# Splitting banded attention probabilities before the turn, and turning them by DMA

## The chip, the cores and the metric

The kernel runs on one core of a Trainium2 chip. A core has five engines with a queue of instructions each: TensorE (PE; its weight loads are shown apart as PEld), VectorE (DVE), ScalarE (ACT), GpSimd (POOL) and SyncE (SP), which here only issues DMAs. An engine works through its queue in order and waits on semaphores for others. The metric is the device time of one launch in microseconds (us), as the median of several runs; lower is better.

## What is computed

One decoder layer on x of 2048 x 1024 floats, with two attention branches side by side. Cut to what matters here:

```python
h = rms_norm(x, g_pre) * (1 + scale) + shift          # scale, shift, gate from silu(c) @ w_ada
qa, ka, va, fa, za, qb, kb, vb, zb = split(h @ w_in)
oa = forgetting_attention(qa, ka, va, fa + b_fgate) * silu(za)      # 8 heads, causal, full length
ob = sliding_window_sink_attention(rope(qb), rope(kb), vb, sinks) * silu(zb)
y  = concat([oa, ob]) @ w_out
out = x + gate * rms_norm(y, g_post)
```

The change is in the second branch, the banded one: 8 query heads, 2 key heads, head size 64. A query of block n (128 queries) sees the 128 keys that end with its own, so keys of blocks n-1 and n, and a learned sink takes part in the softmax but adds no value:

```python
s = q @ k.T / 8                       # 128 queries x 256 keys, per block and head
s = where(band, s, -inf)              # 0 <= i + 128 - j < 128
p = softmax(concat([s, sink]))[:-1]
out = p @ v
```

## The kernel before, in words

Products of floats are made on TensorE from fp16 halves: a number is split into a high half (rounded to fp16) and a low half (the remainder in fp16), and three products (high-high, high-low, low-high) are summed in PSUM.

The work runs in stages. First come the modulation, the normalised input and its first projections. Then comes the stage of the change: from about 139 to 400 us TensorE works off projection units (`punits`, by `fill`, L1185), and between them the banded attention of 32 windows (`Pair`, L932; `windows`, L1182). A window is one pair of query heads and two query blocks, so four blocks of 128 x 128 probabilities. The long causal branch and the output projection follow after the stage.

The order of instructions is written out by hand under a manual schedule. `fill(n)` emits n projection units and what is due at their numbers. `after(n, f)` puts off f by n ticks, and `tick()` (L205) emits what has come due; thus an evacuation by ACT or DVE is put into its queue some units after the matmuls that it waits for. The loop over windows is at L1220. Each turn of it has four parts of projection units (`part`, L1223) and four ticks:

- first tick, then for this window `maxima` (L951): DVE folds the banded scores of 2 blocks x 2 heads, which lie in PSUM, into 128 columns, because each query uses only 128 of its 256 keys (L956), puts in the sink (L958), and takes the row maxima (L961, L963).
- part 0 of the units, then `turn` (L973) for the window before; second tick.
- `exps` (L965): ACT makes four blocks of 128 x 129 exponentials in SBUF in `sm_`, queries on the partitions, with their sums (L970). Part 1, third tick.
- `pv` (L998) two windows back: 24 matmuls (L1005) with the probabilities, keys on the partitions, as stationary operand; later `out_` (L1009) scales by the reciprocal of the sums and stores through `o_store` (L295; ACT high half L307, DVE low half L303, GpSimd issues the store L304 or L297).
- part 2, fourth tick, part 3, then `scores` (L940) of the next window: 12 matmuls (L948) into the single buffer `pss`.
- ACT squares a piece of w_out (L1244) and SP loads the next piece (L1248).

`turn` brings the probabilities to keys on the partitions: TensorE turns the four float32 blocks into the PSUM tile `px` (L977). One tick later (`split`, L985) ACT copies `px` to fp16 as the high half of `fold` (L986), DVE makes the low half as the difference (L987) and the reciprocal of the sums (L989), and GpSimd makes from `fold` the tiles of the two key blocks: four selects (L991, L993) that keep one triangle each and set the other to zero, as the folded columns belong to the previous block above the diagonal and to the own block below it. `fold` and the even windows' result tiles are in the pool `ptp` with one buffer each; odd windows use the pool `stp`. `sm_` is in the pool `sws` with two buffers, `px` in the PSUM pool `ps_t`.

Beside this run in the same stage: the rope of the banded queries (L801 to L829: ACT copy L807, four DMAs on SP that exchange halves L809, DVE products L812, L822, L823, split L826 and L816), the gates (L397: ACT L406, DVE L402, GpSimd store L404), values (L385, L389) and the weight loads and splits (L216 to L293), whose DMAs GpSimd issues.

Much later, at the end of the kernel, the output projection loads stored halves of the attention output with a transposing DMA on SP, 128 x 1024 fp16 each, from DRAM to SBUF (L1555).

Of the kernel before, what the change touches and what calls it, by code (L numbers as in the profile page):

```python
# [10 lines left out]
F32 = mybir.dt.float32  # L11
F16 = mybir.dt.float16
# [3 lines left out]
AF = mybir.ActivationFunctionType  # L16
ALU = mybir.AluOpType
AX = mybir.AxisListType

P = 128  # L20
# [4 lines left out]
CH = 512  # L25
# [18 lines left out]
def hybrid_layer(  # L44
# [17 lines left out]
    V, A, G, PE, SP = nc.vector, nc.scalar, nc.gpsimd, nc.tensor, nc.sync  # L62
# [5 lines left out]
    PSUM = bass.MemoryType.PSUM  # L68
# [14 lines left out]
    def sm(n, tag):  # L83
        return small.tile([P, n], F32, tag=tag, name=tag)
# [70 lines left out]
    ident = const.tile([P, P], F32, name="ident")  # L155
# [46 lines left out]
    def after(n, f):  # L202
        late.append([n, f])

    def tick():  # L205
        now = [f for n, f in late if n <= 1]
        late[:] = [[n - 1, f] for n, f in late if n > 1]
        for f in now:
            f()
# [237 lines left out]
    def turn(ci, k, px=None, us=range(4), hi_a=False):  # L447

        px = px or ps_x.tile([P, CH], F32, tag="x", name="px")

        def turned_(us):
            for u in us:
                PE.transpose(px[:, u * P:(u + 1) * P], xt[ci * 4 + u][:, k * P:(k + 1) * P], ident[:])  # L453

        turned_(us)
        hf = hst.tile([P, CH], F32, tag="hf", name="hf")
        hi, lo = hT[ci][:, 0, k, :], hT[ci][:, 1, k, :]

        def scaled():
            for dst in ([hi] if k % 2 == 0 or hi_a else []) + [hf[:]]:  # L460
                A.activation(dst, px[:], AF.Identity, scale=Gp[:, k:k + 1], bias=Shp[:, k:k + 1])

        def split():
            if k % 2 and not hi_a:
                V.tensor_copy(hi, hf[:])
            V.tensor_tensor(lo, hf[:], hi, op=ALU.subtract)

        return scaled, split, turned_

    def turn_x(ci, k):  # L470
        scaled, split, _ = turn(ci, k)
        after(1, scaled)
        after(2, split)
# [10 lines left out]
    st = start.enter_context(tc.tile_pool(name="start", bufs=1, reuse_waits="tile"))  # L484
# [3 lines left out]
    with ExitStack():  # L488
        rows = st.tile([32, P], F32, name="rows")
# [190 lines left out]
        ada_dve(0, KT - 1, False, 2)  # L680
        ada_sum(0, True)
        turned = [turn(0, k, None, (0, 1)) for k in range(5)]
        squares(0, (2,))
        root(0, slice(2, 3))
# [16 lines left out]
        for u in (2, 3):  # L701
            for k in range(5):
                turned[k][2]((u,))
        turned += [turn(0, k, bk[k - 4]) for k in (5, 6)]
        ku = proj_units("kb", 0, lambda ps, free: kb_units(0, ps, free))
        for k in range(KT):
# [75 lines left out]
    def swa_pool(name, bufs, **kw):  # L782
        return swa.enter_context(tc.tile_pool(name=name, bufs=bufs, reuse_waits="tile", **kw))
# [3 lines left out]
    stp = swa_pool("stp", 2)  # L787
# [144 lines left out]
    class Pair:  # L932
# [39 lines left out]

        def turn(self):  # L973

            px = ps_t.tile([P, 4, P], F32, tag="t", name="pxb")
            for n in range(4):
                PE.transpose(px[:, n, :], self.sm_[:, n, 1:P + 1], ident[:])  # L977
            even = (8 * self.j + self.i // 2) % 2 == 0
            self.ptt = [ptp.tile([P, 2, 4, P], F16, tag=f"pt{b}", name="ptb") if even else
                        stp.tile([P, 2, CH], F16, tag="st", name="ptb") for b in range(2)]  # L980
            ptt = [t[:].rearrange("p a (n c) -> p a n c", n=4) if not even else t[:] for t in self.ptt]
            self.ptt = ptt
            fold = ptp.tile([P, 2, 4, P], F16, tag="fo", name="fold")

            def split():  # L985
                A.activation(fold[:, 0], px[:], AF.Copy)  # L986
                V.tensor_tensor(fold[:, 1], px[:], fold[:, 0], op=ALU.subtract)  # L987
                self.rinv = sm(4, "b_ri")
                V.reciprocal(self.rinv[:], self.rs[:])  # L989
                for n in range(2):  # L990
                    G.affine_select(ptt[0][:, n], fold[:, n], [[0, 4], [-1, P]], ALU.is_ge, 0.0,  # L991
                                    base=-1, channel_multiplier=1)
                    G.affine_select(ptt[1][:, n], fold[:, n], [[0, 4], [1, P]], ALU.is_ge, 0.0,  # L993
                                    base=0, channel_multiplier=-1)

            after(1, split)

        def pv(self):  # L998
            j, i = self.j, self.i
# [182 lines left out]
    windows = [Pair(j, i) for j in range(4) for i in range(0, NB, 2)]  # L1182
    pos = [0]

    def fill(n, each=None):  # L1185

        for _ in range(n):
            for f in events.pop(pos[0], []):
                f()
            punits[pos[0]]()  # L1190
            pos[0] += 1
            if each:
                each()
# [8 lines left out]
    with swa_order:  # L1202
        fill(N_PRO - 4, tick2)
        psx.close()
        sws = swa_pool("sws", 2)
        ptp = swa_pool("ptp", 1)
        ps_s = swa_pool("ps_s", 1, space=PSUM)
        ps_t = swa_pool("ps_t", 1, space=PSUM)
        ps_pv = swa_pool("ps_pv", 1, space=PSUM)
        wsp = swa_pool("wsp", 2)  # L1210
        wss, wst = sm(16, "a_m"), sm(2, "wst")
        wsq = {}
        base = N_PRO
        NW = len(windows)
        windows[0].scores()
        windows[0].maxima()
        fill(2, tick2)
        windows[0].exps()
        fill(2, tick2)
        for n, wd in enumerate(windows):  # L1220
            goal = base + (N_SWA - base) * (n + 1) // NW
            todo = goal - pos[0]
            part = [todo * (m + 1) // 4 - todo * m // 4 for m in range(4)]  # L1223
            tick()
            if n:
                wd.maxima()
            fill(part[0])
            if n:
                windows[n - 1].turn()
            tick()  # L1230
            if n:
                wd.exps()
            fill(part[1])
            tick()
            if n > 1:
                windows[n - 2].pv()
            fill(part[2])
            tick()
            fill(part[3])
            if n + 1 < NW:  # L1240
                windows[n + 1].scores()

            if n:
                A.activation(wsq[n - 1][:], wsq[n - 1][:], AF.Square, accum_out=wss[:, (n - 1) % 16:(n - 1) % 16 + 1])  # L1244
            if n == 16:
                V.tensor_reduce(wst[:, 0:1], wss[:], axis=AX.X, op=ALU.add)
            wsq[n] = wsp.tile([P, 2 * P], F32, tag="wsq", name="wsq")
            SP.dma_start(wsq[n][:], w_out0[n // 4 * P:(n // 4 + 1) * P, n % 4 * 2 * P:(n % 4 + 1) * 2 * P])  # L1248
        tick()
        fill(5)  # L1250
        windows[NW - 1].turn()
        tick()
        fill(5)
        windows[NW - 2].pv()
        tick()
        fill(6)
        windows[NW - 1].pv()
        tick()
        tick()
        A.activation(wsq[NW - 1][:], wsq[NW - 1][:], AF.Square, accum_out=wss[:, 15:16])  # L1260
        V.tensor_reduce(wst[:, 1:2], wss[:], axis=AX.X, op=ALU.add)
        wsum = sm(1, "w_mx2")
        V.tensor_reduce(wsum[:], wst[:], axis=AX.X, op=ALU.add)
# [16 lines left out]
    stp = foxl.enter_context(tc.tile_pool(name="stpa", bufs=3, reuse_waits="tile"))  # L1280
# [432 lines left out]
    with tc.manual_schedule():  # L1713
# [35 lines left out]
        for s, stp_ in enumerate(steps):  # L1749
# [16 lines left out]
            a = b = 0  # L1766
# [102 lines left out]
```

## Time and profile before

| | us |
|---|---|
| median of 3 runs | 1131.02 (1130.87 to 1131.43) |
| the profiled execution | 1129.92 |
| its span, first to last instruction | 1128.2 |
| PE busy in it | 1110.6 |
| DVE busy | 905.6 |
| ACT busy | 656.8 |
| POOL busy | 224.6 |

A line of the timeline holds start and length in us, then engine, line of the kernel, operation, output <- inputs, shapes and how many; in square brackets is the idle time of the engine before it and who ended it. A line of a group holds busy us and the mean of one in ns, then the idle time before. A line of one source line's or tile's view holds the shortest, median and longest of its instructions in ns. Waits are listed as who waited <- for whom: us in total, times, longest. Queue rows end in q (SPq, POOLq): these are issues. DMA rows hold the number, KB of each, and the median us from issue to landing.

### The profile page before, as it was taken

Reading aid. Unit: us, or ns where it says so; the run is one execution under the profiler, and the core shown is the slowest. Engines: PE = TensorE matmul, PEld = TensorE weight load, DVE = VectorE, ACT = ScalarE, POOL = GpSimd, SP = SyncE. Lnnn points to the kernel's source line nnn. Section 1 sums busy time; section 2 is a strip of 40 time slices with the busy share of each in tenths; the row PEclk is TensorE's granted clock in tenths of the full one; section 3 lists DMA queues with packets and bytes.
Section 4 is the critical chain, followed back from the end, with each engine's and each line's share of the span. In section 5 each row is a group of like instructions: output and inputs, shape, how many; then the busy total and the mean of one; then the engine's idle time right before and its main releaser. Section 6 shows DMA issues by size and latency. Waiting matters only on the chain.

```text
span 1128.2 us, 25138 instructions
## 1 busy us (share of the span) xinstructions
PE 1110.6 (98%) x9854; PEld 652.4 (58%) x9854; DVE 905.6 (80%) x1988; ACT 656.8 (58%) x1145; POOL 224.6 (20%) x343
## 2 busy tenths in 40 slices
PE   7899999999999999999999999999999999999997
PEld 2566555676756856556555555655556565544444
DVE  8897488878887468898998989988897997766663
ACT  3974345555555412666766667676666889543332
POOL 3111145545556420010010111001000000100000
PEclk9999999999999999999999999999999999999999
DMA  9854434413333142244223333224311245797632
GB/s 364 280 154 96 81 103 90 93 53 92 83 80 89 39 93 51 65 103 44 58 72 74 86 57 87 51 52 71 72 39 46 76 142 164 153 258 213 193 127 102
DMA packets 124653, 119.77 MB, mean 106 GB/s; under 512 B 66009, under 2 KB 102274, under 8 KB 124534
## 3 DMA queue, kind: packets, MB, share of 16 engines
q1 hardware_dynamic: 113662, 85.66, 28.4%
q0 software_dynamic: 10720, 32.46, 12.6%
q8 instruction: 77, 1.26, 0.6%
q14 instruction: 42, 0.34, 0.1%
q10 hardware_dynamic: 152, 0.04, 0.0%
HBM read 64.43 MB, written 25.18 MB: 79 GB/s over the span
## 4 chain that ended last, share of the span: by engine, by line
PE 83%; DVE 9%; DMA 3%; ACT 3%; issue 2%; SPq 0%; POOL 0%; DVEq 0%; POOLq 0%; ACTq 0%
PE bk L361 32%; PE bk L1650 14%; PE bk L379 7%; PE sta L1414 5%; PE sta L1415 5%; PE bk L1365 5%; PE poa L1440 3%; PE poa L1441 3%; PE poa L1438 3%; PE bk L854 2%; DMA wa<-in_w_ada_dram 2%; PE pss L948 2%; PE pob L1005 1%; PE px L453 1%; DMA xt<-in_x_dram 1%
## 5 line engine op out<-in xcount | busy, mean ns | idle before, releaser
L1421 ACT ACTIVATE p<-sta,lift,scl_qk 128x1024 f32<-128x1024 f32 (+2 forms) x160 | 171.8, 1074 | 128.1 <-PE sta L1415 78.9
L361 PE MATMUL bk<-hT,wh_qk 128*128 128x512 f16 x768 | 196.4, 378 | 0.0
L1428 DVE TENSOR_TENSOR pha<-p,pha 128x1024 f16<-128x1024 f32 (+2 forms) x160 | 168.9, 1056 | 0.2 <-ACT pha L1425 0.2
L1650 PE MATMUL bk<-wohl,oz 128*128 128x512 f16 x744 | 163.2, 379 | 0.0
L1368 DVE TENSOR_REDUCE a_m<-bk 128x1 f32<-128x512 f32 x192 | 130.1, 685 | 37.8 <-PE bk L1365 37.3
L1425 ACT ACTIVATE pha<-p 128x1024 f16<-128x1024 f32 (+2 forms) x160 | 147.8, 924 | 4.9 <-PE poa L1441 0.2
L1650 PEld LDWEIGHTS <-oz 128*128 128x128 f16 x744 | 71.0, 98 | 83.1
L1441 PE MATMUL poa<-vt,pha 128*128 128x65 f16 x1088 | 115.9, 192 | 0.7 <-DVE pha L1428 0.7
L1440 PE MATMUL poa<-vt,pha 128*128 128x64 f16 x1088 | 116.2, 194 | 0.0
L1438 PE MATMUL poa<-vt,pha 128*128 128x65 f16 x1088 | 116.2, 193 | 0.0
L361 PEld LDWEIGHTS <-wh_qk 128*128 128x128 f16 x768 | 71.8, 97 | 73.2 <-issue 1.3
L1414 PE MATMUL sta<-T 128*128 128x512 f16 (+1 forms) x320 | 110.9, 346 | 0.7 <-ACT p L1421 0.7
L1365 PE MATMUL bk<-T 66*128 66x512 f16 (+2 forms) x320 | 110.4, 348 | 0.5 <-DVE a_m L1368 0.2
L1415 PE MATMUL sta<-T 69*128 69x512 f16 (+1 forms) x320 | 109.8, 348 | 0.0
L1438 PEld LDWEIGHTS <-pha 128*128 128x128 f16 x1088 | 101.5, 96 | 14.3 <-issue 0.6
L1440 PEld LDWEIGHTS <-pha 128*128 128x128 f16 x1088 | 100.8, 97 | 11.4
L1441 PEld LDWEIGHTS <-pha 128*128 128x128 f16 x1088 | 100.9, 99 | 0.8 <-DVE pha L1428 0.8
L361 PE MATMUL bk<-hT,wh_za 128*128 128x512 f16 x384 | 100.4, 378 | 0.0
L361 PE MATMUL bk<-hT,wh_zb 128*128 128x512 f16 x384 | 92.1, 379 | 0.0
L379 PE MATMUL bk<-wh_va,hT 128*128 128x256 f16 x768 | 91.9, 273 | 0.0
L361 PE MATMUL bk<-hT,wh_qb 128*128 128x512 f16 x384 | 91.2, 379 | 0.0
L404 POOL DMA_DIRECT2D z_d<-tz x32 | 17.7, 555 | 342.5 <-DVE tz L402 250.9
(463 smaller groups left out, 1956.0 us busy)
## 6 DMA issues: line engine op xcount, KB each, us to landing
hT<-in_x_dram SPq DMA_DIRECT2D x20, 512.0 KB
wa<-in_w_ada_dram SPq DMA_DIRECT2D x16, 512.0 KB
z_d<-tz POOLq DMA_DIRECT2D x32, 256.0 KB, 3.1
T<-z_d SPq DMA_DIRECT2D x16, 512.0 KB
T<-stq SPq DMA_DIRECT2D x60, 128.0 KB
out_dram<-hT SPq DMA_DIRECT2D x15, 512.0 KB
xt<-in_x_dram SPq DMA_DIRECT2D x12, 512.0 KB
qs<-qf SPq DMA_DIRECT2D x80, 64.0 KB
```

Source lines behind the costliest of these rows:

```text
L361: PE.matmul(ps, whl[:, a, k, :], hT[ci][:, b, k, :], start=(k == 0 and n == 0), stop=(k == KT - 1 and n == 2))
L379: PE.matmul(ps[:, (u % 2) * 2 * P:(u % 2 + 1) * 2 * P], hT[ci][:, a, k, u * P:(u + 1) * P], wv[p][:, b, k, :], start=(k == 0 and n == 0), ...
L1365: PE.matmul(mx[:, :w], T[0:XM, 0, i * P:(i + 1) * P], T[0:XM, 2, pc * CH:pc * CH + w], start=True, stop=True)
L1414: PE.matmul(self.st[:, o:o + w], T[:, 3, kb_], T[:, 1, qc], start=True, stop=False)
L1415: PE.matmul(self.st[:, o:o + w], T[0:XR, 2, kb_], T[0:XR, 0, qc], start=False, stop=not diag)
L1421: A.activation(self.p32[:, :self.w], self.st[:, :self.w], AF.Exp, scale=scl[f"qk{self.hd}"][:], bias=lift[:])
L1425: A.activation(self.ph[:, 0, :self.w], self.p32[:, :self.w], AF.Copy)
L1428: V.tensor_tensor(self.ph[:, 1, :self.w], self.p32[:, :self.w], self.ph[:, 0, :self.w], op=ALU.subtract)
L1438: PE.matmul(po[:, u, :], ph[:, 0, pq], vt[:, b, hd, 0:65], start=(self.first and n == 0 and u == 0), stop=False)
L1440: PE.matmul(po[:, u, 0:64], ph[:, 0, pq], vt[:, b, hd, 65:VW], start=False, stop=False)
L1441: PE.matmul(po[:, u, :], ph[:, 1, pq], vt[:, b, hd, 0:65], start=False, stop=(self.last and n == len(self.blocks) - 1))
L1650: PE.matmul(py, self.hl[:, i, k, :], w_slot(8 * j + k)[:, cc], start=(k == 0 and m_ == 0), stop=(k == KT - 1 and m_ == 2))
```

## The change

The order of splitting and turning is exchanged. ACT and DVE now split the probabilities where they lie, with queries on the partitions, into a new SBUF tile `rows_` (128 x 2 x 4 x 128 fp16); one transposing DMA, issued by SP, turns all eight fp16 blocks into `fold`, SBUF to SBUF; the selects read `fold` as before. The transposes on TensorE and their PSUM tile are gone. `turn` is emitted for the same window after the fourth tick, which is two ticks earlier than before; the selects are put off by two ticks in place of one. `sm_` has one buffer in place of two, and `rows_` has one.

```diff
         def turn(self):
 
-            px = ps_t.tile([P, 4, P], F32, tag="t", name="pxb")
-            for n in range(4):
-                PE.transpose(px[:, n, :], self.sm_[:, n, 1:P + 1], ident[:])
             even = (8 * self.j + self.i // 2) % 2 == 0
...
+            rows_ = ptp.tile([P, 2, 4, P], F16, tag="ro", name="rows")
             fold = ptp.tile([P, 2, 4, P], F16, tag="fo", name="fold")
+            sm_ = self.sm_[:, :, 1:P + 1]
+            A.activation(rows_[:, 0], sm_, AF.Copy)
+            V.tensor_tensor(rows_[:, 1], sm_, rows_[:, 0], op=ALU.subtract)
+            SP.dma_start_transpose(fold[:].rearrange("p a n c -> p (a n) c"),
+                                   rows_[:].rearrange("p a n c -> p (a n c)"))
+            self.rinv = sm(4, "b_ri")
+            V.reciprocal(self.rinv[:], self.rs[:])
 
             def split():
-                A.activation(fold[:, 0], px[:], AF.Copy)
-                V.tensor_tensor(fold[:, 1], px[:], fold[:, 0], op=ALU.subtract)
-                self.rinv = sm(4, "b_ri")
-                V.reciprocal(self.rinv[:], self.rs[:])
                 for n in range(2):
                     G.affine_select(ptt[0][:, n], fold[:, n], [[0, 4], [-1, P]], ALU.is_ge, 0.0,
                                     base=-1, channel_multiplier=1)
                     G.affine_select(ptt[1][:, n], fold[:, n], [[0, 4], [1, P]], ALU.is_ge, 0.0,
                                     base=0, channel_multiplier=-1)
 
-            after(1, split)
+            after(2, split)
...
-        sws = swa_pool("sws", 2)
+        sws = swa_pool("sws", 1)
         ptp = swa_pool("ptp", 1)
         ps_s = swa_pool("ps_s", 1, space=PSUM)
-        ps_t = swa_pool("ps_t", 1, space=PSUM)
...
             fill(part[0])
-            if n:
-                windows[n - 1].turn()
             tick()
...
             fill(part[2])
             tick()
+            wd.turn()
             fill(part[3])
...
         fill(5)
-        windows[NW - 1].turn()
         tick()
```

More of the change, by code (lines that the diff above doesn't have):

```diff
@@ L973, in turn @@
         def turn(self):
-            px = ps_t.tile([P, 4, P], F32, tag="t", name="pxb")
-            for n in range(4):
-                PE.transpose(px[:, n, :], self.sm_[:, n, 1:P + 1], ident[:])
             even = (8 * self.j + self.i // 2) % 2 == 0
[L979 to L982, printed above, removed]
+            ptt = [ptp.tile([P, 2, 4, P], F16, tag=f"pt{b}", name="ptb") if even else
+                   stp.tile([P, 2, CH], F16, tag="st", name="ptb") for b in range(2)]
+            self.ptt = ptt = [t[:] if even else t[:].rearrange("p a (n c) -> p a n c", n=4) for t in ptt]
+            rows_ = ptp.tile([P, 2, 4, P], F16, tag="ro", name="rows")
             fold = ptp.tile([P, 2, 4, P], F16, tag="fo", name="fold")
+            sm_ = self.sm_[:, :, 1:P + 1]
[5 more added lines that the diff above has]
+            V.reciprocal(self.rinv[:], self.rs[:])
             def split():
-                A.activation(fold[:, 0], px[:], AF.Copy)
-                V.tensor_tensor(fold[:, 1], px[:], fold[:, 0], op=ALU.subtract)
-                self.rinv = sm(4, "b_ri")
-                V.reciprocal(self.rinv[:], self.rs[:])
                 for n in range(2):
```

## The prediction

> **What bounds the kernel now.** I read the page first: busy shares, slices, the chain that ended last.
>
> ```profile
> span 1128.2 us, 25138 instructions
> PE 1110.6 (98%) x9854; PEld 652.4 (58%) x9854; DVE 905.6 (80%) x1988; ACT 656.8 (58%) x1145; POOL 224.6 (20%) x343
> ...
> PEclk9999999999999999999999999999999999999999
> ...
> PE 83%; DVE 9%; DMA 3%; ACT 3%; issue 2%; SPq 0%; POOL 0%; DVEq 0%; POOLq 0%; ACTq 0%
> ```
>
> TensorE has work in 98% of the span at full clock and carries 83% of the chain. The change lies in one stage, so next I cut that stage out with the windows view, once whole and once from one group of transposes to the next. Columns: span, then busy time of PE, PEld, DVE, ACT, POOL, the clock, the DMA share.
>
> ```profile
> 139.00:400.00 261.00, 260.79 (x2509) 172.17 (x2508) 204.82 (x467) 138.78 (x440) 138.59 (x199) 1.00 0.33 80
> ...
> 157.46:165.56 8.10, 8.10 (x67) 4.58 (x65) 7.80 (x19) 4.53 (x14) 3.70 (x6) 1.00 0.45 116
> ...
> 211.26:219.15 7.89, 7.89 (x92) 6.57 (x91) 7.75 (x14) 4.34 (x15) 4.90 (x8) 1.00 0.32 35
> ...
> 341.80:349.45 7.65, 7.65 (x62) 4.06 (x61) 7.41 (x17) 4.91 (x14) 4.04 (x5) 1.00 0.23 68
> ...
> sum 246.98, PE 246.77 PEld 161.60 DVE 196.06 ACT 134.59 POOL 132.80; mean PE 7.71 PEld 5.05 DVE 6.13 ACT 4.21 POOL 4.15
> ```
>
> PE idles 0.2 us in 261, so time taken off PE here shortens the stage as long as the others keep up, and no more than that 0.2 us can be won beside it. VectorE is the one that may not keep up: on average 6.13 of 7.71 us, but nearly full in some intervals (7.75 of 7.89). ScalarE and GpSimd are little over half full.
>
> **What goes: the transposes.** The timeline shows what one group of four costs PE, from its start to the start of the next matmul.
>
> ```profile
> 150.33 0.60 PE L977 MATMUL pxb<-ident,sm__1861 128*128 128x128 f32 x4
> 150.76 4.05 PE L361 MATMUL bk<-hT,wh_zb 128*128 128x512 f16 x18
> ...
> 389.38 0.60 PE L977 MATMUL pxb<-ident,sm__5678 128*128 128x128 f32 x4
> 389.82 0.93 PE L379 MATMUL bk<-wh_va,hT 128*128 128x256 f16 x7
> ```
>
> That is 0.43 to 0.44 us (the 0.60 shown includes the pipeline's end). There are 32 groups, first and last shown, 31 intervals of (389.38 - 150.33)/31 = 7.71 us. Gain: 32 x 0.43 = **13.8 us**, and an interval becomes 7.28 us if PE still sets it.
>
> **What changes sides: copy and subtract.** The fp16 copy (ACT) and the remainder (DVE) used to read PSUM; they now read the probabilities in SBUF. The nearest rows with an SBUF source of 512 floats a partition are the rope's (L816, L822, L826); the --lines view gives the means.
>
> ```profile
> L986 ACT ACTIVATE fold<-pxb x32: 587/597/597, 151.0 to 390.1; 128x512 f16<-128x512 f32 x32
> L987 DVE TENSOR_TENSOR fold<-pxb,fold x32: 674/682/692, 153.4 to 391.6; 128x512 f16<-128x512 f32 x32
> L816 DVE TENSOR_TENSOR stb<-qc,stb x15: 660/693/1732, 149.4 to 360.9; 128x512 f16<-128x512 f32 x15
> L826 ACT ACTIVATE stb<-qc x15: 629/630/640, 148.5 to 360.3; 128x512 f16<-128x512 f32 x15
> ```
> ```profile
> L822 DVE TENSOR_TENSOR qs<-qs,sinT 128x512 f32<-128x512 f32 x15 | 17.2, 1144 | 0.0
> L816 DVE TENSOR_TENSOR stb<-qc,stb 128x512 f16<-128x512 f32 x15 | 13.3, 884 | 1.2 <-ACT stb L826 1.1
> ```
>
> ACT pays 0.63 for 0.60 us, nothing beside 45% idle time. For DVE the median is the same 0.69, but some instances take 1.73 us; these operands are in SBUF, where GpSimd works too, while the PSUM form never exceeds 0.69. So the subtract costs between 0.01 and 0.46 us more (884 and 1144 are the two means); I take L816's, of the same types: 0.884 - 0.683 = 0.20 us. Twelve of the 31 intervals (first, heaviest of the early ones and last are quoted) then hold more DVE work than their own length less 0.43 us, by 0.1 to 0.5 us each, 4.3 us together; with no extra cost it is ten intervals and 2.0 us. Where half a microsecond of lag is taken up by the next, lighter interval, 1.1 us is left. There is a second charge: the subtract now stands in DVE's queue behind the same window's exponentials.
>
> ```profile
> 207.27 0.46 ACT L970 ACTIVATE sm__2801<-pss,b_nb,scl_qb 128x129 f32<-128x129 f32 x1 [0.65 <-DVE b_nb L963]
> ...
> 208.94 0.20 ACT L970 ACTIVATION_READ_ACCUMULATOR sm__2801<-pss,b_nb,scl_qb 128x1 f32 x1
> ```
>
> Four exponentials take 1.87 us and the copy 0.63, so DVE cannot begin it before 2.5 us after the first of them; whatever stands behind (gating, rope, the next maxima) waits. In light intervals that falls into idle time, in heavy ones DVE usually comes later than that anyway. Bounds for all of DVE: 0 to 8 us; I take **3.0 us**. A gain is excluded, since PE has no other idle time to give.
>
> **What comes: the transposing DMA.** The trace before holds the same instruction, 128 x 1024 fp16, at the kernel's end, with DRAM as its source.
>
> ```profile
> L1555 SPq DMA_TRANSPOSE T<-o_d x24: 1242/1514/3602, 959.7 to 1069.0; - x24
> ```
> ```profile
> 1036.27 2.90 SPq L1555 DMA_TRANSPOSE T<-o_d  x2
> ```
> ```profile
> DMA packets 2199, 0.61 MB, mean 205 GB/s; under 512 B 2128, under 2 KB 2184, under 8 KB 2199
> ```
> ```profile
> L304 POOL DMA_DIRECT2D o_d<-oh x24: 755/763/782, 184.6 to 402.7; - x24
> ...
> DMA to landing us min/median/max: 2.2/2.9/7.2
> ```
> ```profile
> z_d<-tz POOLq DMA_DIRECT2D x32, 256.0 KB, 3.1
> ...
> out_dram<-hT SPq DMA_DIRECT2D x15, 512.0 KB
> ...
> wr_qb<-in_w_in_dram POOLq DMA_DIRECT2D x4, 512.0 KB, 5.4
> ```
>
> It holds SP's queue 1.24 to 3.60 us. The small packets of the pair issued at 1036.27 all pass between 1038.0 and 1041.0 (the DMA view of that stretch; a 512 KB store went ahead of them): about 1.4 us of data each. Its landing is not shown; the nearest rows are 3.1 us (same 256 KB) within 2.2 to 7.2. I take 3.1.
>
> Who waits for it? GpSimd's selects, then PE's product L1005. The turn now stands half an interval (3.6 us) ahead of the selects, which `after(2)` leaves at their old tick; copy, subtract and DMA take 0.63 + 0.88 + 3.1 = 4.6 us, so the selects may start 1.0 us late. L1005 follows five quarters of an interval (9.1 us) after that tick: 1.0 and the four selects leave over 5 us. GpSimd stands waiting at that place anyway, for DVE ahead of its store:
>
> ```profile
> POOL o_d L304 <- DVE oh L303: 74.7, 23, 5.5
> ```
>
> (us in total, times, longest.) Tighter is the loop through the single `fold`: the next DMA may not write before the four selects of this window have read.
>
> ```profile
> L993 POOL TENSOR_SCALAR_AFFINE_SELECT ptb<-fold 128x512 f16<-128x512 f16 x64 | 48.2, 753 | 0.0
> L991 POOL TENSOR_SCALAR_AFFINE_SELECT ptb<-fold 128x512 f16<-128x512 f16 x64 | 46.2, 721 | 21.9 <-ACT fold L986 17.1 <-DVE fold L987 4.5
> ```
>
> 2 x (0.753 + 0.721) = 2.95 us; with 3.1 the loop takes 6.05 us, under 7.28. Cost 0, covered by PE's matmuls; it shows from a landing of 4.33 us on. The transpose waits in SP's queue for the subtract, and behind it stand the rope's exchange (L809) and the w_out load (L1248).
>
> ```profile
> 151.16 2.42 SPq L809 DMA_DIRECT2D qs<-qf  x4
> 153.62 1.08 SPq L1248 DMA_DIRECT2D wsq<-in_w_out_dram  x2
> ...
> 165.96 2.42 SPq L809 DMA_DIRECT2D qs<-qf  x4
> ```
> ```profile
> 160.51 2.12 DVE L822 TENSOR_TENSOR qs<-qs,sinT 128x512 f32<-128x512 f32 x1
> ```
>
> The exchange is issued by 153.58 and needed at 160.51: 6.9 us, less a hold of up to 3.60, still leaves time to land. The w_out load can no longer run a window ahead (now two go out at once), but its squaring stands a whole window later. Cost 0. One buffer of `sm_` instead of two adds no wait: the next exponentials need `b_nb`, which DVE makes behind the subtract. The reciprocal only moves; the selects and all other DMAs stay.
>
> **Sum.** 1129.92 (profiled execution; span 1128.2 and 1.72 around it) - 13.8 + 3.0 = 1119.1. The median before is 1.1 above that execution: **1120.2 us**.
>
> **Weighed against the Trainium skill.** In the trace a pair of 128 x 1024 transposes is moved in under 3 us. The Trainium skill, "VectorE: DVE Perf Modes", section "The three transpose paths", gives 1309 ns for one 128 x 128 bf16 block by DMA against 390 ns on TensorE, and its rules keep TensorE where a PSUM destination will do. Eight blocks at that price would be an estimated 10.5 us a window, a loop of 13.4 us, and some 1308 us in all; the trace's 1.4 us per eight blocks does not agree, so I do not use it.
>
> **Rivals.**
> 1. DVE becomes the bound. If the subtract costs L822's 1.144 us (+0.46), the twelve heavy intervals overrun by 7.5 us; with 0.25 us each for the wait behind the exponentials it is 10.5. Gain 3 to 6 us: 1124 to 1128.8. For it: 7.75 of 7.89 us. Against: most heavy intervals have a lighter one beside them, the mean being 6.13, and the median subtract costs nothing more.
> 2. Slower: the fold loop sets the pace. At the longest hold of the trace plus the data, 3.60 + 1.4 = 5.0 us to landing, the loop is 7.95 us; against 7.71 before, 31 x 0.24 = 7.4 us: 1138.4. It beats the old time only below 4.76. At the longest landing seen, 7.2, it would be 1207. For it: the stage's DMA share is 0.33 and 512 KB weight loads run beside it. Against: the transposes at the end stand behind 512 KB stores and half of them still hold SP no longer than 1.5 us. Of its chance, 0.03 is for 1200 us and beyond.
> 3. Nothing to measure: gains and losses cancel within 0.2% (2.3 us, about what a measurement of this kernel tells from no change).
>
> **Numbers.** Forecast (1117 to 1124): 0.58; rival 1: 0.17; rival 3: 0.05; rival 2: 0.20. Faster 0.75, same 0.05, slower 0.20. Range 1116 to 1133: the first three, from the full 13.8 (1117.2) with PE's 0.2 and the spread of the runs below it, up to the edge of "same"; the slower rival is left out.
>
> **What would show it.** Right: no L977; groups of four fewer on PE and about 7.3 to 7.4 us from one window to the next; 32 transposes on SP in the stage holding 1.2 to 1.6 us; GpSimd's first select waiting little for the DMA; the stage ending some 11 us earlier and all after it shifted unchanged. Rival 1: PE idle until DVE frees a bank, in the heavy intervals only, and a subtract near 1.1 us. Rival 2: GpSimd idle on the DMA in every window, SP on GpSimd, PE idle ahead of L1005. I am wrong altogether if PE's intervals shrink by 0.43 us and the time is given back after 400 us.

## The result, and the profile after

The changed kernel takes 1186.71 us (median of 6 runs, 1184.54 to 1191.27) against 1131.49 (6 runs, 1130.87 to 1134.39): a ratio of 1.0495, 95% interval 1.048 to 1.0511. It is 5% slower, and the forecast was 1% faster.

The page of the changed kernel's profiled execution, the lines that answer to those of before:

```profile
span 1184.8 us, 25007 instructions
PE 1121.7 (95%) x9726; PEld 646.0 (55%) x9726; DVE 908.6 (77%) x1988; ACT 658.7 (56%) x1145; POOL 228.0 (19%) x343
...
PEclk9999998999997999999999999999999999999999
...
PE 67%; DMA 15%; DVE 8%; POOL 4%; issue 3%; ACT 2%; SPq 0%; POOLq 0%; DVEq 0%; ACTq 0%
```

TensorE's 128 transposes are gone (x9854 to x9726), but its share of the chain fell from 83% to 67%, and DMA has 15% of it where it had 3%. The same marker, the DMA that SP issues at the end of the stage, stands at 398.62 us before (first row, kernel before) and at 454.91 after (second row, changed kernel):

```profile
398.62 2.10 SPq L1316 DMA_DIRECT2D T<-crow  x3
```
```profile
454.91 2.13 SPq L1313 DMA_DIRECT2D T<-crow  x3
```

From the marker to the end it is 729.6 us before and 729.9 after. So the loss lies in the stage: 56.3 of the 56.6 us between the two profiled executions. The waits of the changed kernel in it (who waited <- for whom: us in total, times, longest):

```profile
POOL ptb L991 <- DMA fold<-rows: 96.1, 26, 8.8
DVE rows L983 <- ACT rows L982: 68.3, 23, 9.5
ACT rows L982 <- DMA fold<-rows: 60.0, 21, 8.6
...
PE pob L1005 <- POOL ptb L991: 26.1, 17, 3.7
...
ACT wsq L1242 <- DMA wsq<-in_w_out_dram: 15.2, 8, 3.8
```

From TensorE backwards: it waits at the product for GpSimd's selects, GpSimd for the transposing DMA, ScalarE's copy for the DMA too (it may not overwrite `rows_` while that is read), VectorE's subtract for the copy, and the DMA for the subtract. The critical view of the changed kernel from 340 to 358 us shows what turns in a circle there:

```profile
344.61 10.31 DMA fold<-rows
...
355.08 0.62 POOL ptb L991
355.70 0.49 issue
...
356.25 1.08 POOL ptb L991
357.33 0.60 POOL ptb L993
357.92 0.02 issue
357.94 11.35 DMA fold<-rows
```

DMA, four selects, next DMA, with nothing of TensorE between: the loop through the single `fold`. The first transpose is issued at 151.0 and the last at 445.1, so a window takes (445.1 - 151.0)/31 = 9.49 us, where it took 7.71. SP is held 1.25 us by each, as forecast; the landing is what differs. From issue to the first engine that was waiting for it, it takes 3.2 us at least, 11.4 at most, 5.2 in the median and 6.2 in the mean (30 windows in which someone waited).

What makes one long? The timeline of the window at 344.61 (changed kernel), and the DMA view of the 5.2 us before it lands at 355.0:

```profile
344.61 1.25 SPq L984 DMA_TRANSPOSE fold<-rows  x1
...
344.99 0.57 POOL L239 DMA_DIRECT2D mx_d<-w_mx  x1 [0.41 <-DVE w_mx L236]
...
347.12 0.77 POOL L304 DMA_DIRECT2D o_d<-oh  x1 [1.56 <-DVE oh L303]
...
355.00 0.63 ACT L982 ACTIVATE rows<-sm__4518 128x512 f16<-128x512 f32 x1 [6.52 <-DMA fold<-rows]
```
```profile
DMA packets 0, 0.00 MB, mean 0 GB/s; under 512 B 0, under 2 KB 0, under 8 KB 0
```

All packets had passed by 349.8, and nothing moved from there to 355.0. So this is no lack of bandwidth: the transfer is over and its completion comes 5 us later. Beside it GpSimd had sent the maxima of a weight block to DRAM, 0.5 KB. Windows sorted by what GpSimd issued within 1.5 us before and 2 us after the transpose: an ordinary store 3.2 to 5.0, median 3.8 (10 windows); that 0.5 KB store 4.6 to 10.6, median 8.5 (8); a 256 or 512 KB load 5.6 to 11.4, median 8.2 (6). The other six take 4.6 to 6.0; five of them stand beside the 64 KB load that fetches the maxima back. The two long groups are not alike: beside the small store the transpose's packets are through 2.6 to 3.7 us after its issue and only the completion is late, beside a load its packets themselves last until 3.6 to 6.6 us.

### The profile page after: what moved, and what is told of

Its sections match the earlier page's. It is cut to its first block, busy times and chain, and to the rows that moved or that the text cites. A ratio compares the mean times of both kernels' runs of the same rounds, so it can differ in the third digit from the quotient of the medians.

```text
span 1184.8 us, 25007 instructions
## 1 busy us (share of the span) xinstructions
PE 1121.7 (95%) x9726; PEld 646.0 (55%) x9726; DVE 908.6 (77%) x1988; ACT 658.7 (56%) x1145; POOL 228.0 (19%) x343
## 3 DMA queue, kind: packets, MB, share of 16 engines
q8 instruction: 76, 1.25, 0.5%
## 4 chain that ended last, share of the span: by engine, by line
PE 67%; DMA 15%; DVE 8%; POOL 4%; issue 3%; ACT 2%; SPq 0%; POOLq 0%; DVEq 0%; ACTq 0%
PE bk L361 26%; PE bk L1647 13%; DMA fold<-rows 11%; PE sta L1411 5%; PE sta L1412 5%; PE bk L1362 4%; PE poa L1437 3%; PE poa L1438 3%; PE poa L1435 3%; POOL ptb L991 2%; POOL ptb L993 2%; PE bk L854 2%; DMA wa<-in_w_ada_dram 1%; PE bk L379 1%; PE px L453 1%
## 5 line engine op out<-in xcount | busy, mean ns | idle before, releaser
L1437 PEld LDWEIGHTS <-pha 128*128 128x128 f16 x1088 | 100.8, 97 | 11.4
L361 PE MATMUL bk<-hT,wh_zb 128*128 128x512 f16 x384 | 97.7, 400 | 0.7 <-DVE qc L812 0.7
L361 PE MATMUL bk<-hT,wh_qb 128*128 128x512 f16 x384 | 94.6, 396 | 0.0
```

The costliest lines, as they stand in the source:

```text
L361: PE.matmul(ps, whl[:, a, k, :], hT[ci][:, b, k, :], start=(k == 0 and n == 0), stop=(k == KT - 1 and n == 2))
L1437: PE.matmul(po[:, u, 0:64], ph[:, 0, pq], vt[:, b, hd, 65:VW], start=False, stop=False)
```

## The experiments

Two questions: is the loss the new order of work or the wait for the DMA, and what makes the landing long. One run each, beside a run of the kernel before on the same chip, unless runs are named (that kernel: 1129.97 for x1 to x4, 1130.17 for x5 to x8, 1131.16 for x9 to x16). The edits are against the changed kernel if nothing else is said.

**x1: without the DMA.**

```diff
-            fold = ptp.tile([P, 2, 4, P], F16, tag="fo", name="fold")
+            fold = rows_
-            SP.dma_start_transpose(...)
```

> Leaves the turn out: no transposing DMA, the selects read the split tile where it is, everything else as in the changed kernel. Theory (the DMA lands too late): with no landing to wait for, the stage falls to PE's own work, 1131 - 13.8 + 0 to 5 us, so 1117 to 1122 us. Rival (the new places of copy and subtract, DVE waiting behind ACT, are what costs): the time stays above 1150 us.

1150.02 us: a miss. The DMA is worth 36.7 us, but 20 us of loss are left without it. With one tile for both, ScalarE's copy waits for the selects of the window before (34.7 us in 20 windows), and VectorE's subtract for the copy (41.2 us).

**x2: a plain DMA of the same bytes.**

```diff
-            SP.dma_start_transpose(fold..., rows_...)
+            SP.dma_start(fold[:], rows_[:])
```

> The transposing DMA replaced by a plain DMA of the same 256 KB between the same two tiles, so the probabilities are not turned; all waits stay. Theory (it is the transposing kind, with its 256-byte packets, that lands late beside other traffic): the plain one lands in about 3 us and the time is 1117 to 1125 us. Rival (any DMA of this size in this loop lands too late, because the queues are busy): 1160 us or more. Landing of 5 us or more in most windows would speak for the rival.

1154.11 us: 4 above no DMA at all and 33 below the transposing one. So neither range held. Its landings are 2.5 to 9.7 us, median 3.7 (16 windows in which someone waited); the two longest, 8.9 and 9.7, stand beside the 0.5 KB store.

**x3: two sets of tiles.** The split tile gets two buffers, and the DMA writes into the result tile, which alternates with the window.

```diff
-            rows_ = ptp.tile(..., tag="ro", name="rows")
-            fold = ptp.tile(...)
+            rows_ = ptp.tile(..., tag="ro", name="rows", bufs=2)
+            fold = ptt[1]
```

> The split tile gets two buffers, and the turned tile is one of the two result tiles (the second select overwrites it in place), so it alternates between two places; no transpose has to wait for the selects or the copy for the transpose of the window before. Theory a (the loop through the single buffers sets the pace: landing + 3 us of selects): most of the loss goes, 1120 to 1140 us. Theory b (a single landing of 8 to 11 us is by itself later than PE's product two windows on, whatever the buffers): it stays above 1150 us.

1151.59 us, in the range of theory b; still, 35.1 us come back although the same DMA is waited for, because a late landing no longer stops the next copy. GpSimd still waits 40.4 us for the DMA, and ScalarE 30.4 us for the w_out load that is queued behind it.

**x4: pairs of DMAs by themselves.** 

> A kernel that holds only DMAs, each case five times, each round starting when all of the round before has landed (its output is not the layer's): a transposing DMA of 128 x 1024 fp16 in SBUF alone, beside a 512 KB weight load of GpSimd's queue, behind the same load on SP's own queue, beside a 256 KB store of GpSimd's queue; and a plain DMA of the same bytes in the same company. Theory (its packets wait in turn with the large packets of the other queue): alone 3.2 us to landing, beside GpSimd's load 7 to 11 us, beside the store 4 to 6, behind SP's load about the load's 5.5 us or a little more; the plain DMA stays within 2 us of its time alone. Rival (plain shortage of bandwidth): plain and transposing DMA are stretched alike, and by no more than the load's own 1.5 to 2 us of data.

Alone the transpose lands after 3.0 to 3.2 us, the plain copy after 2.2 to 2.3. Beside a 512 KB load of GpSimd's queue 3.1 to 5.0 and 2.2 to 2.3; beside GpSimd's 256 KB store 4.5 to 4.6 and 2.3; the transpose behind a load on SP's own queue 4.4 to 4.6. So my 3.1 us was right for a DMA with nothing beside it, and the 7 to 11 us of the theory did not come. Which kind is stretched is not shown: GpSimd's load and store were issued 0.3 to 1.9 us behind the DMA, and the plain copy, which needs 0.8 us less, can have been through before they moved data (x13 has both kinds behind their neighbour).

**x5 and x6: the order without the DMA.** Both leave it out and split into the alternating result tile; x6 also moves copy and subtract behind the next window's maxima, with two buffers of `sm_`.

```diff
-            rows_ = ptp.tile(...); fold = ptp.tile(...)
+            fold = rows_ = ptt[1].rearrange("p a n c -> p a n c")
-            SP.dma_start_transpose(...)
# x6 only:
-        sws = swa_pool("sws", 1)
+        sws = swa_pool("sws", 2)
                 wd.maxima()
+                windows[n - 1].turn()
...
-            wd.turn()
```

> As x1 without any DMA (probabilities not turned), but the split is written into one of the two result tiles, which alternate, so no copy waits for the selects of the window before; the order of copy, subtract and maxima is that of the changed kernel. Theory (ring: the next maxima stand behind the subtract on DVE, the subtract behind the copy, the copy behind the exponentials on ACT, and the next exponentials behind the maxima, so the two engines no longer work beside each other): still slow, 1138 to 1152 us, exponentials waiting some 50 us for the bias from DVE. Rival (x1 was slow only because its single tile made ACT wait 35 us for the selects): 1117 to 1124 us.

> x5 with one thing moved: copy and subtract of a window are emitted right behind the maxima of the next one (as before the change, where they stood one tick behind them), with two buffers for the exponentials; no DMA, probabilities not turned. Ring theory: the wait of the exponentials falls back to about the 18.5 us of before and the time to 1117 to 1123 us, PE's own work. Rival (the SBUF operands themselves, beside GpSimd, slow DVE): within 5 us of x5.

x5 1132.83 us, x6 1122.32. TensorE's longest waits in the stage, four of x5 (all of them the next scores, which wait for the exponentials) and then two of x6:

```profile
PE pss L948 <- ACT sm__2750 L970: 2.9, 1, 2.9
PE pss L948 <- ACT sm__2171 L970: 2.4, 1, 2.4
PE pss L948 <- ACT sm__4794 L970: 2.3, 1, 2.3
PE pss L948 <- ACT sm__2403 L970: 1.9, 1, 1.9
```
```profile
PE pss L948 <- ACT sm__2746 L970: 1.8, 1, 1.8
PE pob L1002 <- POOL ptb L990: 1.6, 3, 0.7
```

x5 is 17.2 us faster than x1, as no copy waits there for the selects of the window before, and lies between its two ranges. The 10.5 us between x5 and x6 come from the order and `sm_`'s second buffer together, which were changed at once. The explanation offered is a ring over two engines: the next maxima stand behind this window's subtract (VectorE), the subtract behind the copy, the copy behind the exponentials (ScalarE), the exponentials behind their own maxima, so that VectorE and ScalarE work in turn instead of side by side. It is argued, not shown. For it: TensorE's waits for the exponentials fall. Against it: the sign named beforehand, a wait of the exponentials for VectorE's `b_nb` that falls back to 18.5 us, did not come. Both in the view of `b_nb`, first x5 (the exponentials' wait for `b_nb`, then TensorE's for the exponentials), then x6:

```profile
  DVE b_nb L963: 54.7, 25
  PE pss L948: 12.4, 9
```
```profile
  DVE b_nb L963: 58.5, 30
  PE pss L948: 3.6, 4
```

x6 also shows what the change could be worth, 7.9 us.

**x7: x6's order with the DMA.** One split tile, the turned tile alternating, the selects two ticks behind.

> x6 with the transposing DMA back: copy and subtract behind the next maxima, the turned tile alternating between two places, one buffer for the split, selects two ticks later, so the full layer with the turn on the DMA. Ring theory with landings of 3 to 8 us: 1118 to 1135 us, below the kernel before if most landings stay under 5 us. Rival (landing is what matters most, and there is less time for it here): above 1145 us, PE waiting for the selects in most windows.

1162.38 us, 40 us above x6. GpSimd waits 71.8 us for the DMA (24 windows), ScalarE's copy 26.5, TensorE 19.5 for the selects.

**x8: the DMA alone.** The kernel before, with a transposing DMA of the same size in each window that nobody reads.

```diff
         def turn(self):
+            junk = ptp.tile([P, 8, P], F16, tag="ro", name="unread")
+            SP.dma_start_transpose(junk[:], vb[:, 0:4].rearrange("p a n c -> p (a n c)"))
-        sws = swa_pool("sws", 2)
+        sws = swa_pool("sws", 1)
```

> The kernel before, with a transposing DMA of the same size per window added on SP, from constant data into a tile that nobody reads (one buffer for the exponentials to make room). Theory (the DMA itself takes no time from anyone, only waiting for it does): 1131 to 1135 us. Rival (its packets hold up the other queue's loads and stores, the rope's exchange and the w_out loads, and these hold up ACT and DVE): 1140 us or more, with ACT waiting for w_out loads.

1130.18 us against 1130.17. In the old order the DMA's load on queues and engines costs nothing, and nor does one buffer of `sm_`; what costs in the change is what waits for the landing, and the new order.

**x9 and x10: weight loads on SP.** The weight loads that GpSimd issues in the stage go to SP's queue (`sp_loads` is filled for the length of the stage); x9 from the changed kernel, x10 from x3.

```diff
-            (eng or G).dma_start(raw[:, :, o:o + n], ...)
+            (eng or (SP if sp_loads else G)).dma_start(raw[:, :, o:o + n], ...)
```

> The changed kernel with one thing moved: the weight loads that GpSimd issues in this stage are issued by SP instead, so that no 512 KB load runs beside a transpose on another queue unless SP put it there. Theory (the landing of the transpose stretches while another queue's transfer is under way, and the single tiles turn that into time): landings fall from a median of 5.3 us towards 3.1 to 4.5, the waits for them (156 us on GpSimd and ScalarE together) fall by a third or more, and the time comes to 1150 to 1172 us. Rival (the landing is long because of the stores and of other traffic, whatever the queue; or the loads now stand behind SP's waits and come late): 1180 us or more, landings still above 5 us, and DVE's maxima of the weights wait for the loads.

> x3_two_sets (split tile in two buffers, turned tile alternating with the window, in place of its result) with the weight loads issued by SP. Theory: x3 lost 19 us to the no-DMA form of the same order (1151.6 against 1132.8) through landings of 4.5 us median and 7.5 at most; with landings nearer 3.1 to 4.4 it comes to 1138 to 1147. Rival (the landing is not the loads' doing): 1150 or more. A third outcome: the loads come late behind SP's waits for the subtract, PE waits for weight halves, 1155 or more.

x9 1164.48 us, x10 1152.18. With single tiles 22 us come back; the windows beside a load are gone from the long ones, those beside the 0.5 KB store still take 7.8 to 10.2 (6 windows). With two sets the loads make no difference, so x10's theory fell.

**x11: two half DMAs.** x3 with the high halves sent behind the copy, the low ones behind the subtract.

> x3_two_sets with the transposing DMA cut in two, the high halves sent behind ScalarE's copy and the low halves behind VectorE's subtract. If a window's landing is data time, the high half lands before the low one is ready and only half the data is left behind the subtract: landing of the second about 2.4 us alone, time 1142 to 1149 us. If it is a fixed time for each transposing DMA, and SP is held 1.2 us by each of them, the second lands no sooner and the time is 1151 to 1160.

1157.74 us, 6 more than x3, in the range of the second branch. Each half holds SP as long as the whole did (1.21 us in the median), so the run tells that halving does not pay, and not how much of a landing is data time.

**x12: one tick later.** x7 with the loads on SP and `after(3, split)`.

> x7_late_dma (copy, subtract and DMA behind the next window's maxima) with the selects three ticks behind the turn in place of two, and the weight loads issued by SP. x6, the same without a DMA, took 1122.3. Theory (all that x7 lost over x6, 40 us, is GpSimd standing at the first select for the landing, 72 us in all, and the stores and loads behind it in its queue): with 1.8 us more slack and fewer transfers beside it the wait falls under 20 us and the time to 1126 to 1145. Rival (a window is turned too close to its product, so that a later select only moves the wait to TensorE): 1155 or more, with TensorE waiting for the selects.

1150.73 us. The median landing is 3.0, but five of 28 take 5.7 to 9.3, four of them with a 0.5 KB store sent up to 4 us earlier or 2 us later, and GpSimd waits 67.5 us in all: neither theory had it.

**x13: the small store by itself.** 

> DMAs alone, no layer is computed. What the transpose of 128 x 1024 fp16 takes to land beside the other kinds of DMA that GpSimd issues in the stage: the 0.5 KB store of 128 maxima, at the same time and 1.5 us before; the same small store issued by SP or by ScalarE; a 512 KB load sent 2 us before; each of the three on GpSimd with a plain copy for comparison. Theory (a transposing DMA reports itself done only behind the DMAs of GpSimd that were under way when it was sent, and the small store takes long): landing with the small store near 8 to 10 us, 1.5 us less with the lag, near 5 beside the load; plain copy 2.3 to 3. Rival (the long landings of the layer come from its queues being full, not from a partner): all cases 3.1 to 3.4.

The landings of the probe's cases, from its DMA view (the last figure is the median from issue to landing):

```profile
dst_c_tiny<-src SPq DMA_DIRECT2D x5, 256.0 KB, 2.4
dst_c_tiny_lag<-src SPq DMA_DIRECT2D x5, 256.0 KB, 5.6
dst_c_load_lag<-src SPq DMA_DIRECT2D x5, 256.0 KB, 3.6
md<-zt POOLq DMA_DIRECT2D x25, 0.5 KB, 7.3
...
dst_t_tiny<-src SPq DMA_TRANSPOSE x5, 9.2
dst_t_tiny_lag<-src SPq DMA_TRANSPOSE x5, 5.9
md<-zt SPq DMA_DIRECT2D x5, 0.5 KB, 6.9
dst_t_sptiny<-src SPq DMA_TRANSPOSE x5, 6.7
dst_t_atiny<-src SPq DMA_TRANSPOSE x5, 7.7
md<-zt ACTq DMA_DIRECT2D x5, 0.5 KB, 7.4
dst_t_load_lag<-src SPq DMA_TRANSPOSE x5, 3.7
```

One pair in the timeline and in the DMA view of 68 to 80 us (40 slices of 0.3 us):

```profile
68.31 1.36 SPq L48 DMA_TRANSPOSE dst_t_tiny<-src  x1
68.64 0.54 POOL L66 DMA_DIRECT2D md<-zt  x1 [4.65 <-DVE zt L60]
77.50 0.54 POOL L69 DMA_DIRECT2D back_t_tiny<-md  x1 [8.32 <-DMA md<-zt]
77.51 0.15 DVE L74 CAST mark<-dst_t_tiny 128x1 f32<-128x1 f16 x1 [9.17 <-DMA dst_t_tiny<-src]
```
```profile
DMA  0000049999000000000000000000000000000003
```

The data of the transpose is through by 71.3 us. It is reported done at 77.5, in the moment in which the small store is, with no packet between; the store's own packets had passed by 70.5. The store takes 6.9 to 7.4 us in the median whoever issues it, and the transpose waits for it on any queue. The plain copy is held as well when it comes 1.5 us behind the store (5.6, where the transpose takes 5.9), but lands in 2.4 when both start together. That need not be a difference in kind: its packets are through 2.0 us after issue and those of the transpose 2.7 to 2.8, while the store's pass until 2.1 to 2.7 us, so the copy may simply have gone first. The DMA views of 202 to 206 us (copy issued at 202.62, store at 202.94) and of 270 to 274 us (the store's packets pass first, at 270.5, and the copy's follow), in slices of 0.1 us:

```profile
DMA  0000000000000000008999899420000000000000
```
```profile
DMA  0000010000000000000288999961000000000000
```

That fits x2, whose landings are shorter in the median and still reach 9.7. Behind a load sent 1.6 to 1.9 us ahead the transpose lands in 3.7, the plain copy in 3.6, and not in the 8.2 of the kernel, so what holds the windows beside loads is not reproduced by a pair.

**x14 to x16: no small store in the stage.** The maxima go over the partitions by TensorE (one 128 x 128 transpose a block, into the bank that `px` had) in place of DRAM, which takes away both the 0.5 KB store and the 64 KB load back. x14 from the changed kernel, x15 from x10, x16 from x12. What it comes to in the stage:

```diff
-        G.dma_start(md[:], mx[:])
+        V.tensor_copy(mxr[:], mx[:].broadcast_to([P, P]))
...
-        G.dma_start(mxr[:], md.rearrange("p o -> (p o)").partition_broadcast(P))
+        PE.transpose(pt[:], mxr[:], ident[:])
+        after(1, lambda: V.tensor_reduce(mx2[:], pt[:], axis=AX.X, op=ALU.max))
```

> The changed kernel with one thing exchanged: the row maxima of the projections' weights no longer go through DRAM in this stage (0.5 KB store and 64 KB load back, both on GpSimd); TensorE turns a broadcast copy instead, into the PSUM bank that the change set free. Theory (the small store holds back the landing of a transpose that is sent beside it: 8.5 us median in 8 windows, against 3.8 beside an ordinary store): about 8 x 4.7 = 38 us of waits less, of which the stage gives back most, so 1150 to 1165 us. Rival (those windows would have waited for something else anyway): 1178 or more.

> x10_two_sets_loads_on_sp with the exchange of maxima by TensorE as in x14. Theory: no landing over 5 us is left, the waits for landings and for the w_out load fall from 39 and 27 us to under 15 each, and the time comes near the no-DMA form of the same order, 1132.8: 1133 to 1142. Rival: 1148 or more, the same as x10.

> x12_late_three_ticks with the exchange of maxima by TensorE as in x14: the order without a ring, three ticks of slack, no small store and no large load of GpSimd beside a transpose. Theory: landings 3 to 5 us, time between the no-DMA form x6 (1122.3) and the kernel before: 1124 to 1134. Rival (GpSimd, which issues the stores in order behind its selects, and TensorE, which needs a window's probabilities one and a half intervals after its exponentials, stay late whatever the landing): 1140 or more.

x14 1162.28 us (24.4 less than the changed kernel), x15 1136.04 (16.1 less than x10), x16 1130.71 (20.0 less than x12), each in the range of its theory. In x14 the only landings above 5.1 us are the six beside loads (6.4 to 9.7, median 8.6); in x16 none of 26 is above 4.7. GpSimd had stood only 6.2 us for the small store itself in the changed kernel, so it is mainly the landings that give the time back. The first rows of x14's waits, against those of the changed kernel above:

```profile
POOL ptb L1013 <- DMA fold<-rows: 65.6, 19, 7.4
...
DVE rows L1005 <- ACT rows L1004: 42.6, 18, 7.5
ACT rows L1004 <- DMA fold<-rows: 30.8, 12, 6.9
```

**x17: x16 with the selects two ticks behind,** in 11 runs. 

> x16_no_small_store_late with the selects two ticks behind the turn again, as in x7. x16 left 5.6 us of TensorE's waits for the selects, and GpSimd stands at the first select for the landing in 25 of 32 windows either way, so an earlier place in its queue costs nothing and lets the last two selects come earlier. Theory: 1124 to 1129 us, faster than the kernel before by 0.2% or more. Rival (GpSimd's earlier wait delays the stores behind it and ScalarE and VectorE with them): 1131 or more.

1130.13 us (1128.82 to 1132.35) against 1130.19 (15 runs): ratio 1.0, interval 0.9991 to 1.0009. The theory fell; the waits of TensorE for the selects are 6.5 us, where x16 has 5.6:

```profile
PE pob L1029 <- POOL ptb L1017: 5.4, 9, 1.1
PE pss L972 <- ACT sm__2768 L994: 1.2, 1, 1.2
PE pob L1029 <- POOL ptb L1015: 1.1, 1, 1.1
```

The stage ends 3.2 us earlier than before (marker at 395.39), and 2.7 us of that are given back behind it (732.3 us in place of 729.6).

**x18: the kernel before with the exchange by TensorE.** Here the 128 x 128 transpose shares the bank with `px`, as no other is free. Five runs. 

> The kernel before, with TensorE's transposes, and with only the exchange of maxima taken from DRAM to TensorE as in x14, so that what this brings by itself can be taken off x16 and x17. Theory (nobody waits there for a landing that the small store could hold back): 1130 to 1133 us, no difference; a gain of more than 2 us would mean that part of x16's recovery has nothing to do with the transposing DMA.

1148.69 us, ratio 1.0166 (1.0153 to 1.018): a miss. TensorE waits 6.5 us until the reduction of the maxima has left the shared bank, and 5.4 until the bank is free for the maxima. So it shows no gain of the exchange by itself, but it is not a clean measure of its price in a bank of its own.

## Why the prediction was wrong

**What held.** The stage, and nothing behind it, changes. 32 groups of transposes leave TensorE, SP is held 1.25 us each, and the unread DMA costs nothing (x8). With no landing to wait for, and with copy and subtract behind the next maxima, the layer gains 7.9 us (x6, 1122.3 against 1130.2), where -13.8 and +3.0 gave 10.8: their sum is within 3 us in that order. The subtract took 0.68 to 1.62 us in the changed kernel, 1.04 in the mean: 0.36 us more than before, within the bounds of 0.01 to 0.46 but not the 0.20 that was taken.

**The step that failed: "I take 3.1 ... Cost 0, covered by PE's matmuls; it shows from a landing of 4.33 us on."** The loop was the right one, the landing was not. 3.1 is what the DMA takes alone (x4); the row that gave it was the median of 32 stores of the same size. In the kernel the mean is 6.2; by the forecast's own loop, 31 x (6.2 + 2.95 - 7.71) = 45 us, against 56.3 measured. Rival 2 was therefore the right mechanism, and its chance of 0.20 and its price of 1138.4 came from a landing of 5.0, hold plus data; it also priced the longest landing seen, 7.2, at 1207, and gave 0.03 to 1200 us and beyond. The row against it was "half of them still hold SP no longer than 1.5 us": a hold is not a landing. A completion that comes 5 us behind the last packet stood in the trace before as well, at the 0.5 KB store: in the stage its packets pass within 1.3 to 1.9 us of issue and it lands after 6.8 to 8.1. I read only the rows of similar size:

```profile
mx_d<-w_mx POOLq DMA_DIRECT2D x23, 0.5 KB, 7.3
```

Nothing in that trace says that one DMA holds back another's completion; x13 was needed for that. The Trainium skill, "Advanced Engine Details and Errata", section "X-Bar Transpose (TRN2)", states that transpose DMAs are as fast as regular ones. The probe does not agree for a DMA with nothing beside it: 3.1 us against 2.3 for the plain copy. Behind the small store the two are nearly alike, 5.9 against 5.6.

**"One buffer of `sm_` ... adds no wait: the next exponentials need `b_nb`, which DVE makes behind the subtract."** The wait is not free in the new order: copy and subtract ahead of the next maxima, with one buffer, cost 10.5 us (x5 against x6), more than the 0 to 8 allowed for all of DVE, while one buffer in the old order costs nothing (x8). TensorE waits 12.4 us for the exponentials in x5 and 3.6 in x6. The prediction had both halves of the ring, the subtract behind the exponentials and the next exponentials behind the subtract, but priced only the first. That the ring is the cause stays open, as said at x6.

**The single `rows_`** was not in the forecast at all: the copy waits for the DMA's read of the window before, 60.0 us in the changed kernel. x3, which doubles it and lets the turned tile alternate, gets 35.1 us back; the two tiles were not separated. The sum had put this wait at nothing.

**"The w_out load ... Cost 0"** failed too: ScalarE waits 15.2 us for it, and 30.4 in x3, since the load stands behind the transpose in SP's queue. What that is worth in time was not measured by itself.

**How the 55.2 us divide.** Not by a sum, as the causes work through the same single tiles: taking away the DMA gives 36.7, the small store with its load back 24.4, the loads beside it 22.2, single tiles 35.1, by one run each. In the best order with everything taken away that was found (x17), the change comes to no difference. x17 stays 7.8 us above x6. Between the profiled executions (spans 1127.7 and 1120.6) it is 7.1: the stage ends 4.0 us later (x6's marker is at 391.35), with waits of TensorE for the selects of 6.5 us where x6 has 1.6, and the part behind it takes 732.3 us where x6 has 729.3. Why the part behind the stage grew stays open (it is 732.3 to 735.0 in x14 to x17 and 729.3 to 732.2 in the runs that keep the small store, but 730.3 in x18), and so does what holds a landing beside a load.

## What to carry to other kernels

A DMA put between engines costs its time to completion, and in this kernel that was set by what else was in flight: look at the longest landings in the trace, the smallest transfers among them, and not at rows of the same size. Before a wait is called covered, follow each single buffer around its loop with that time, and follow each queue around as well: a new order of two engines' work through one window cost time here (10.5 us) although no engine was full. Here the store of 128 single floats to DRAM was the neighbour to move first.

## What was not expected of the hardware

- A 0.5 KB store of 128 single floats to DRAM takes 6.9 to 7.4 us in the median whoever issues it (GpSimd, SP, ScalarE). A transposing DMA in flight with it completes 0.2 us behind it in 16 of 20 rounds of x13, and 1.7 to 2.6 us behind it in the others: 9.2 us in place of 3.1 when both start together, 5.9 when it starts 1.5 us later.
- The hold is not one of the transposing kind alone: a plain copy of the same 256 KB that starts 1.5 us behind that store takes 5.6 us. Started together with it, it lands in 2.4, its packets being through 0.7 us earlier than the transpose's.
- What is sent behind the two is held as well: the 128 KB store issued at 347.12 landed after 10.7 us, where the median before was 2.9.
- In the stretch in which TensorE has gaps its granted clock is lower too, so that more time is lost than the gaps. The trace shows eight spells at half clock there, of 3.4 or 6.8 us, 41 us together; each begins in a gap of 1.4 us or more or within 2 us of its end, but not every such gap has one. The window of the changed kernel from 139 to 455 us, clock third from the end (1.00 before):

```profile
139.00:455.00 316.00, 269.61 (x2377) 164.82 (x2376) 206.62 (x463) 139.45 (x437) 140.85 (x198) 0.94 0.47 91
```

The stretch is 55.0 us longer. TensorE is idle for 46.4 us of it, and busy 269.6 us where the 260.8 of before less the transposes' 13.8 would be 247.0.
